# Mixture of experts by nested seven-product multiplication: the turn from P6 to P7 and P4 is put in another order, with operands and one weight sum kept on chip

## The chip, the cores and the metric

The kernel runs on one core of one Trainium2 chip. The metric is device time in microseconds (us) of one execution. The profile is a hardware trace of one execution; "PE" is the matrix engine (TensorE), "DVE" the vector engine, "ACT" the scalar engine, "POOL" GpSimd and "SP" the sync engine. ACT, POOL and SP also issue DMA transfers, each from its own queue of instructions, in order.

## The reference

Each of 8192 tokens (16 batches of 512) is multiplied with the weights of all eight experts, and the eight results are added with the softmax of the token's router logits as factors:

```python
    logits_max = np.max(router_logits, axis=-1, keepdims=True)
    probs = np.exp(router_logits - logits_max)
    probs = probs / np.sum(probs, axis=-1, keepdims=True)
    ...
    for e in range(n_experts):                      # 8 experts
        expert_out = np.matmul(x, expert_weights[e])    # [.., 512] x [512, 2048]
        output += probs[:, :, e:e+1] * expert_out
```

With the factors put on the tokens, this is one product of an 8192 x 4096 matrix (token times factor, for the 512 inputs of each of 8 experts) with a 4096 x 2048 matrix of all weights.

## The kernel before, in words

The large product is cut in two in each direction: the rows into even and odd blocks of 256 tokens, the inner dimension into experts 0 to 3 and 4 to 7, the columns into a left and a right half of 1024. Instead of eight block products the kernel makes seven (the scheme of Strassen in Winograd's form), named P1, P2, P5, P6, P7, P4 and P3 after the number `r` that `product(r, q)` takes. For each of them 16 row pairs `q` = 0 to 15 are worked through; a pair is the token blocks `a` = 2q and `b` = 2q + 1. Inside, each `Product` is cut in the same way once more, which gives seven steps of eight matmuls (`STEPS`: 1, 5, 6, 2, 7, 3, 4).

Left operands (class `Left`). Tiles `z` of 128 x 2048 elements, two for each product (`t[0]`, `t[1]`), are made on DVE. `times` multiplies a token block by factors; P6's left operand is P5's minus the block a's own; P7's is block a's product minus block b's (`first`, `second`, `less`: three instructions of DVE for each of two tiles, lines 433 to 453). Beside them a difference `d` (`queue_s2`) and a combination `i` (`queue_i`, queued when the stage begins) are made.

Right operands (class `Right`). Seven weight tiles of 1 MB, numbered by step. The weights of P7 and P4 are kept in DRAM (tiles `wd`): `by_parts` (line 1049) loads a quarter of the four raw blocks, makes the four sums 5, 7, 6 and 4 in place on DVE (`sums_in_place`, line 1010) and writes them back, four times for each. For P4 each raw block first has t2 subtracted (`less_t2`), and the difference is written back too before the sums run over it. `turnover` (line 1104) then fetches the seven tiles one by one from ACT's queue, three steps apart.

Results. A result tile `h` is 128 x 512 in f32. Four of them make up one product's result; each is added on DVE from a PSUM bank (or copied by ACT) and stored by POOL (`to_out`). P7 adds onto what P6 stored: `Base` loads the four tiles back from the output by SP's queue (`fetch_at` in line 911), the first three in the stage before their use and the fourth at step 3 of the stage itself. P4 then adds onto P7's tiles and lets the DMA accumulate into the output.

Order. `add` appends a stage of one or two products; a stage of two has 14 steps, in turns. The stages around the change are: (6, q) with (5, q + 1) for q = 1 to 14; then stage k7 with (6, 15) and (7, 0); then (4, q) with (7, q + 1) for q = 0 to 14; then k3 with (4, 15) and (3, 0). Work beside the matmuls is hung to a stage and a step by `at`. DVE's instructions are put in order by a planner: `later` appends a task with an estimated cost to a queue, `slack` runs tasks while the estimated time of DVE is behind that of PE, and `need` forces a task when a step reads it. DVE, ACT, POOL and SP execute what they are given in that order. Waits, and the choice of buffers, are put in by the framework; the pools hold 15 weight tiles (`w`), 8 `z`, 13 `h` and 9 of token blocks and factors (`xT`, `pT`). Each queue's DMA may wait for an earlier DMA, of this or another queue, that counts on the same semaphore.

Of the kernel before, what the change touches and what calls it, by code (L numbers as in the profile page):

```python
# [31 lines left out]
def kernel(  # L32
# [17 lines left out]
    C = H // P  # L50
# [60 lines left out]
    def tt(o, a, b, op):  # L111
        dve(nc.vector.tensor_tensor(out=o, in0=a, in1=b, op=op))  # L112
# [229 lines left out]
    class Task:  # L342


        def __init__(self, cost, make):
            self.cost, self.make, self.done = cost, make, False
# [79 lines left out]
    class Left:  # L426


        def __init__(self, xb, pb, less=None, of=None, part=None):
            self.xb, self.pb, self.less, self.of, self.part = xb, pb, less, of, part  # L430
            self.t, self.task, self.s2, self.i = [None, None], {}, None, None

        def makes(self, k):

            def first():
                if self.of is not None:
                    need(self.of.task[k])
                self.t[k] = new_z()
                times(self.t[k], k, self.xb, self.pb)

            def second():
                self.u = new_u()
                times(self.u, k, *self.less)

            def less():
                t = self.t[k]
                if self.of is not None:
                    tt(t, self.of.t[k], t, SUB)
                else:
                    tt(t, t, self.u if self.part is None else self.part.t[:, k], SUB)  # L450
            if self.less is not None:
                return first, second, less
            return (first, less) if self.of or self.part else (first,)
# [12 lines left out]
            self.task["s2"] = later(0.61, make)  # L466

        def queue_i(self):
            def make():
                self.i = new_z()  # L470
                two = "p k (h t) -> p h k t"
                tt(self.i.rearrange(two, h=2), self.t[1].rearrange(two, h=2),
                   self.s2.unsqueeze(1).to_broadcast([P, 2, K8, HP]), SUB)
            self.task["i"] = later(1.14, make)
# [174 lines left out]
    def out_rows(q, odd, cols, tn):  # L649
        t, n = tn  # L650
        return out_f[ds((2 * q + odd) * HQ + t * HP, HP), ds(cols * NH + n * NB, NB)]
# [26 lines left out]
    def add(*products):  # L678
        stages.append(products)
        return len(stages) - 1  # L680
# [7 lines left out]
    def xblock(h):  # L688
        if h not in xs:
            xs[h] = XBlock(h)  # L690
        return xs[h]

    def left_of(r, q, fresh=True):
        a, b = 2 * q, 2 * q + 1
        if r == 1:
            pt = PBlock(a, P1, xp1[q - 2][1] if q in (2, 3) else None)
            if q in (2, 3):
                xs[a] = XBlock(a, xp1[q - 2][0])
            return Left(xblock(a), pt), [xblock(a), pt]
        if r in (2, 4):  # L700
            h, pt = (a, PBlock(a, P2)) if r == 2 else (b, PBlock(b, P2))
            return Left(xblock(h), pt), [xblock(h), pt]
        if r == 5:
            pt = PBlock(b, PQ)
            return Left(xblock(b), pt), [xblock(b), pt]
        if r == 6:
            pt = PBlock(a, P1)
            return Left(xblock(a), pt, of=lefts[5, q]), [xblock(a), pt]
        if r == 3 and q in KEEP:
            pt = PBlock(a, P2)  # L710
            return Left(xblock(a), pt, part=Operand(lefts[6, q].kept)), [xblock(a), pt]
        pa, pb = PBlock(a, P1 if r == 7 else PQ), PBlock(b, P1 if r == 7 else PQ)
        return Left(xblock(a), pa, (xblock(b), pb)), [xblock(a), pa, xblock(b), pb]

# [2 lines left out]

    def product(r, q, **how):
        left, loads = left_of(r, q)
        lefts[r, q] = left  # L720
        p = None
        if r == 1:
            def sink(tn, o):
                pool(kept_rows(q)(tn), o)
            p = Product(right[1], left, sink)
        elif r == 2:
            if q >= 9:
                base = products[1, q].o.__getitem__
            else:
                base = bases[2, q] = Base(kept_rows(q))  # L730
            p = Product(right[2], left, to_out(q, 0, 0), base)
        elif r == 5:
            bases[6, q] = m1 = Base(kept_rows(q))
            m1.task = {}

            p = Product(right[5], left, to_out(q, 1, 0))
        elif r == 6:
            m1 = bases[6, q]

            def base(tn):  # L740
                need(m1.task[tn])
                return m1.t[tn]
            p = Product(right[6], left, to_out(q, 0, 1), base)
            if q in KEEP:
                left.kept = dram.tile([P, 2, K8, HQ], f16, name=f"kept_left_{q}")
        elif r == 7:
            base = bases[7, q] = Base(lambda tn: out_rows(q, 0, 1, tn))
            p = Product(right[7], left, to_out(q, 1, 1), base)
        elif r == 4:
            p = Product(right[4], left, to_out(q, 1, 0, accum_op=ADD), products[7, q].o.__getitem__)  # L750
        else:
            p = Product(right[3], left, to_out(q, 0, 1, accum_op=ADD), **how)
        p.loads = loads
        products[r, q] = p
        return p
# [21 lines left out]
                    load.store()  # L777

    def queue_left(left):
        if not left.task:  # L780
            left.queue_make(0)
            left.queue_s2()
            left.queue_make(1)

    thirds, splits, held = {}, {}, []

# [75 lines left out]
    def fetch_at(stage, slot, base, *tns):  # L862
        for tn in tns:
            at(stage, slot, lambda tn=tn: base.fetch(tn))
# [18 lines left out]
        add(product(6, q), product(5, q + 1))  # L883
    some = product(6, 15)
    xs.clear()
    k7 = add(some, product(7, 0))
    for q in range(15):
        add(product(4, q), product(7, q + 1))
    some = product(4, 15)
    xs.clear()  # L890
    k3 = add(some, product(3, 0))
    add(product(3, 14), product(3, 15))
# [1 line left out]
        add(product(3, q), product(3, q + 1))  # L894
    end = add(product(3, 13))
    late[k3 - 1] = 6

    def joined(q, tn):
        m1 = bases[6, q]
# [2 lines left out]
    for q in range(16):  # L902
        k = k5 + 1 + q
        duo = len(stages[k - 1]) == 2
        for slot, tn in zip((2, 4, 6, 8) if duo else (1, 2, 3, 4), INNER):
            fetch_at(k - 1, slot, bases[6, q], tn)
        for tn, where in zip(INNER, ((k - 1, 12), (k - 1, 13), (k - 1, 13), (k, 3)) if duo
                             else ((k - 1, 5), (k - 1, 6), (k - 1, 6), (k, 3))):
            at(*where, lambda q=q, tn=tn: joined(q, tn))
        for slot, tn in zip((7, 9, 11, 17), INNER):  # L910
            fetch_at(k7 + q - 1 + slot // 14, slot % 14, bases[7, q], tn)


    def wedge(kn, e):
# [92 lines left out]
            pool(kept_w("t4", ODD), made.pop(21))  # L1007
        later(2.2, make)

    def sums_in_place(part, b, r, cost):  # L1010

        def one(p, o, x, y):
            def make():
                tt(o, x, y, SUB)
                part(p, o)
            return later(cost, make)
        one(5, b[0, 0], b[0, 1], b[0, 0])
        one(7, b[0, 1], b[1, 1], b[0, 1])
        one(6, b[1, 1], b[1, 1], b[0, 0])
        return one(4, b[1, 0], b[1, 0], b[1, 1])  # L1020

    last2 = k5 - 1
    for stage, slot, q in ((9, 9, 12), (10, 2, 11), (10, 9, 22), (last2, 8, 21)):
# [25 lines left out]
    def by_parts(stage, slot, every, r, load, between, when):  # L1049

        for j in range(4):
            b, chunks = {}, ds(2 * j, 2)

            def begin(b=b, j=j, chunks=chunks):
                flush(last_part[0])
                t = new_w()
                for i, kn in enumerate(ORDER):
                    b[kn] = t[:, ds(2 * i, 2), :]
                    load(b[kn], kn, j, chunks)

            def go_on(b=b, chunks=chunks):
                for kn in b:
                    if kn != ODD:
                        between(b[kn], kn, chunks)

            def end(b=b, chunks=chunks):
                last_part[0] = sums_in_place(lambda p, o: pool(part_of((r, p), (0, 0), chunks), o), b, r, 0.61)
            at(*slots_after(stage, slot, j * every), begin)
            if between is not None:
                at(*slots_after(stage, slot, j * every + when[0]), go_on)  # L1070
            at(*slots_after(stage, slot, j * every + when[-1]), end)
# [23 lines left out]
        pool(part_of("b22", kn, chunks), t)  # L1095

    by_parts(k5 + 2, 4, 14, 7, load_part("t3"), None, (7,))
    by_parts(*slots_after(k5 + 2, 4, 60), 24, 4, load_p4, less_t2, (8, 15))
    by_parts(k7 + 4, 4, 36, 3, cast_part(22), keep_raw, (9, 16))


# [2 lines left out]
    def turnover(stage, place, r, raw):  # L1104
# [8 lines left out]
        at(stage - 1, 9, lambda: fetch(1))  # L1113
        for i, p in enumerate(STEPS[1:]):
            at(*slots_after(stage, place + 1, 3 * i), lambda p=p: fetch(p))
    turnover(k7 - 1, 1, 7, "t3")
    turnover(k7, 0, 4, "t4")
    turnover(k3 - 1, 1, 3, "b22")


# [94 lines left out]
```

## Time and profile before

| | us |
|---|---|
| median of three runs | 1374.11 |
| lowest and highest run | 1373.30 and 1378.75 |
| profiled execution | 1372.54 |
| its span, first to last instruction | 1370.8 |
| PE busy | 1362.6 (99%) |
| DVE busy | 1121.1 (82%) |
| POOL busy | 411.4 (30%) |
| ACT busy | 193.7 (14%) |

Between the span and the profiled execution's time lie 1.7 us. The 6610 matmuls are pipelined: one of 512 columns lasts 376 ns in the records, and the next begins before it has ended. Busy time of PE therefore tells that there was no gap, and the count of matmuls in a stretch tells the pace. The granted clock of TensorE is 1.000 over the span. A group of the costliest instructions carries line 112 or 132, since helpers issue all of DVE's and PE's; the tiles' names tell them apart.

### The profile page before, as it was taken

To read this page: it belongs to the slowest core of one execution; us is meant where nothing else is said; L and a number is where in the kernel's file an instruction comes from. 1 tells how busy PE (TensorE), PEld (TensorE's weight loads), DVE (VectorE), ACT (ScalarE), POOL (GpSimd) and SP (SyncE) were. 2 spreads that over 40 slices of the span, in tenths; PEclk is the share of its full clock that TensorE was granted. 3 is DMA by queue.
4 is the path that set the end of the run, shared out by engine and by line. 5 is a ranking of instruction groups with operands and counts; after the bars stand their busy time and mean duration, and the time that the engine had idled before them with its cause. 6 is when DMAs were issued, how large, how long until landed. Compare 5 with 4: busy or idle time off the path is not lost.

```text
span 1370.8 us, 18076 instructions
## 1 busy us (share of the span) xinstructions
PE 1362.6 (99%) x6610; PEld 644.1 (47%) x6610; DVE 1121.1 (82%) x1359; ACT 193.7 (14%) x354; POOL 411.4 (30%) x652
## 2 busy tenths in 40 slices
PE   8999999999999999999999999999999999999999
PEld 4455444444444444444444444444444444456554
DVE  5868757689889888798887978888889798997873
ACT  3232111100011111111111100000000000123321
POOL 3222333331223343343332112242332422233232
PEclk9999999999999999999999999999999999999999
DMA  9898999999897999999998999889797979999896
GB/s 182 217 223 245 208 237 283 233 323 358 235 340 245 323 295 332 286 318 315 306 296 289 364 371 258 200 236 209 227 264 216 242 212 282 309 209 241 203 207 121
DMA packets 193161, 358.50 MB, mean 262 GB/s; under 512 B 53168, under 2 KB 87216, under 8 KB 187696
## 3 DMA queue, kind: packets, MB, share of 16 engines
q0 software_dynamic: 88688, 185.12, 56.1%
q1 hardware_dynamic: 98336, 130.15, 31.3%
q10 hardware_dynamic: 6048, 42.08, 8.3%
q8 instruction: 51, 0.84, 0.2%
q14 instruction: 38, 0.31, 0.1%
HBM read 214.47 MB, written 170.07 MB: 281 GB/s over the span
## 4 chain that ended last, share of the span: by engine, by line
PE 74%; issue 11%; DMA 9%; POOL 4%; DVE 1%; ACT 0%; SPq 0%; POOLq 0%; DVEq 0%
PE ps L132 74%; DMA out_dram<-h 4%; POOL out_dram L126 2%; DMA wd<-w 2%; DMA xs<-in_x_dram 2%; DMA xT<-xs 1%; POOL wd L126 1%; POOL w L126 1%; DMA w<-in_expert_weights_dram 0%; DVE h L112 0%; DVE z L112 0%; POOL xs L126 0%; SPq L397 0%; POOLq L126 0%; DVE z L234 0%
## 5 line engine op out<-in xcount | busy, mean ns | idle before, releaser
L132 PE MATMUL ps<-w,z 128*128 128x512 f16 (+1 forms) x5272 | 1136.1, 376 | 1.7 <-DMA w<-in_expert_weights_dram 1.2
L132 PEld LDWEIGHTS <-z 128*128 128x128 f16 x5344 | 522.7, 98 | 607.2 <-DVE h L112 1.5
L126 POOL DMA_DIRECT2D out_dram<-h x380 | 249.1, 661 | 722.6 <-ACT h L559 365.4
L112 DVE TENSOR_TENSOR h<-ps,h 128x512 f32<-128x512 f32 x415 | 283.1, 686 | 177.1 <-PE ps L132 159.2
L112 DVE TENSOR_TENSOR z<-xT,pT 128x2048 f16<-128x2048 f16 x220 | 266.8, 1216 | 13.8 <-DMA xT<-xs 11.4
L132 PE MATMUL ps<-w,d 128*128 128x512 f16 x880 | 199.1, 379 | 0.4 <-DVE ps L112 0.4
L132 PEld LDWEIGHTS <-d 128*128 128x128 f16 x880 | 86.1, 98 | 102.5 <-issue 0.7
L112 DVE TENSOR_TENSOR z<-z,d 128x2048 f16<-128x2048 f16 x110 | 131.5, 1215 | 0.0
L112 DVE TENSOR_TENSOR w<-w 128x1024 f16<-128x1024 f16 (+2 forms) x92 | 100.7, 1102 | 9.2 <-DMA wd<-w 5.0
L559 ACT COPY h<-ps 128x512 f32<-128x512 f32 x64 | 37.5, 586 | 480.6 <-PE ps L132 458.8
L548 ACT COPY h<-ps 128x512 f32<-128x512 f32 x90 | 52.8, 586 | 326.5 <-PE ps L132 292.4
L112 DVE TENSOR_TENSOR d<-z 128x1024 f16<-128x1024 f16 x110 | 74.7, 686 | 7.6 <-PE ps L132 6.0
L112 DVE TENSOR_TENSOR ps<-ps,h 128x512 f32<-128x512 f32 (+1 forms) x102 | 60.3, 595 | 19.5 <-PE ps L132 19.3
L545 ACT COPY h<-ps 128x512 f32<-128x512 f32 x90 | 52.0, 589 | 151.7 <-PE ps L132 148.8
L126 POOL DMA_DIRECT2D wd<-w x86 | 48.6, 587 | 45.5 <-DVE w L112 34.7
L126 POOL DMA_DIRECT2D w<-in_expert_weights_dram x65 | 48.4, 761 | 28.0 <-DMA wd<-w 17.9
L126 POOL DMA_DIRECT2D kept<-h x56 | 30.8, 549 | 70.3 <-ACT h L548 40.0
L112 DVE TENSOR_TENSOR z<-z,u 128x2048 f16<-128x2048 f16 x38 | 46.1, 1214 | 0.1
L112 DVE TENSOR_TENSOR u<-xT,pT 128x2048 f16<-128x2048 f16 x38 | 46.2, 1215 | 0.0
L112 DVE TENSOR_TENSOR h<-h 128x512 f32<-128x512 f32 (+2 forms) x69 | 45.0, 674 | 0.1
L541 ACT COPY ps<-ps 128x512 f32<-128x512 f32 x45 | 25.6, 570 | 104.0 <-PE ps L132 98.2
L112 DVE TENSOR_TENSOR z<-z 128x2048 f16<-128x2048 f16 x32 | 39.0, 1220 | 0.6
(60 smaller groups left out, 262.8 us busy)
## 6 DMA issues: line engine op xcount, KB each, us to landing
out_dram<-h POOLq DMA_DIRECT2D x380, 256.0 KB, 6.7
pT<-p_dram SPq DMA_DIRECT2D x127, 256.0 KB, 6.5
w<-wd ACTq DMA_DIRECT2D x27, 1024.0 KB, 9.2
h<-kept SPq DMA_DIRECT2D x100, 256.0 KB, 7.9
xT<-x SPq DMA_DIRECT2D x74, 256.0 KB, 6.6
wd<-w POOLq DMA_DIRECT2D x72, 256.0 KB, 6.2
w<-in_expert_weights_dram POOLq DMA_DIRECT2D x35, 512.0 KB, 9.5
h<-out_dram SPq DMA_DIRECT2D x68, 256.0 KB, 5.5
```

Of the source, the lines that this page charges most:

```text
L112: dve(nc.vector.tensor_tensor(out=o, in0=a, in1=b, op=op))
L126: note(nc.gpsimd.dma_start(out=o, in_=i, **how))
L132: note(nc.tensor.matmul(ps, z, w, start=start, stop=stop, skip_group_check=True))
L541: act(nc.scalar.copy(self.banks["b"], x))
L545: act(nc.scalar.copy(o[tn], q if p == 5 else x))
L548: act(nc.scalar.copy(o[TN[p]], b if p == 2 else x))
L559: act(nc.scalar.copy(o[tn], b))
```

## The change

The diff moves and removes work around the turn to P7 and P4. PE's instructions are the same, in number and in shape.

1. Row pairs 14 and 15 come first in P7 and P4 (`order7`), ahead of 0 to 13, so that k7 holds (6, 15) and (7, 14), and the next stage (4, 14) and (7, 15). For these two pairs P7 adds onto P6's result tiles as they stand in SBUF (`products[6, q].o`), with no load of a base.
2. For these two pairs P7's left operand is made from P6's, in P6's own tiles (`into`): block b's token product for experts 4 to 7 goes into `u`, and P6's tile is subtracted from it in place. `queue_into` queues the first tile and the difference at step 6 of the stage before, the second tile is queued by `queue_i` when the stage begins.
3. For P7 and P4 `sums_in_place` makes three sums (5, 7, 6), not four. The fourth is made on chip from the fetched tiles 2 and 6 by `turnover_with_sums`, in two halves on DVE, ahead of the other tasks in the queue; six tiles are fetched rather than seven.
4. The quarters of P4's weights begin 28 steps apart, not 24, and their sums are queued 19 steps after the begin, not 15.

```diff
+            def all_of_it():
+                self.u = new_u()
+                times(self.u, k, self.xb, self.pb)
+
+            def less_in_place():
+                need(self.into.task[k])
+                t = self.t[k] = self.into.t[k]
+                tt(t, self.u, t, SUB)
+            if self.into is not None:
+                return all_of_it, less_in_place
...
         def queue_i(self):
+            if self.into is not None:
+                self.queue_make(1)
...
+        if r == 7 and q >= 14:
+            pt = PBlock(b, P2)
+            return Left(xblock(b), pt, into=lefts[6, q]), [xblock(b), pt]
...
         elif r == 7:
-            base = bases[7, q] = Base(lambda tn: out_rows(q, 0, 1, tn))
+            if q < 14:
+                base = bases[7, q] = Base(lambda tn: out_rows(q, 0, 1, tn))
+            else:
+                base = products[6, q].o.__getitem__
...
+    def queue_into(left):
+        left.queue_make(0)
+        left.queue_s2()
...
-    k7 = add(some, product(7, 0))
-    for q in range(15):
-        add(product(4, q), product(7, q + 1))
-    some = product(4, 15)
+    order7 = [14, 15, *range(14)]
+    k7 = add(some, product(7, order7[0]))
+    for q, next_q in zip(order7, order7[1:]):
+        add(product(4, q), product(7, next_q))
+    some = product(4, order7[-1])
...
+    for k, q in ((k7, 14), (k7 + 1, 15)):
+        at(k - 1, 6, lambda q=q: queue_into(lefts[7, q]))
...
-        for slot, tn in zip((7, 9, 11, 17), INNER):
-            fetch_at(k7 + q - 1 + slot // 14, slot % 14, bases[7, q], tn)
+        if q < 14:
+            for slot, tn in zip((7, 9, 11, 17), INNER):
+                fetch_at(k7 + q + 1 + slot // 14, slot % 14, bases[7, q], tn)
...
-        one(6, b[1, 1], b[1, 1], b[0, 0])
-        return one(4, b[1, 0], b[1, 0], b[1, 1])
+        sixth = one(6, b[1, 1], b[1, 1], b[0, 0])
+        return one(4, b[1, 0], b[1, 0], b[1, 1]) if all_ else sixth
...
-    by_parts(*slots_after(k5 + 2, 4, 60), 24, 4, load_p4, less_t2, (8, 15))
+    by_parts(*slots_after(k5 + 2, 4, 60), 28, 4, load_p4, less_t2, (8, 19))
...
+    def turnover_with_sums(stage, place, r, raw):
+
+        w = right[r].w = {}
+
+        def fetch(p):
+            w[p] = fetch_w(raw, RAW[p]) if p in RAW else fetch_w((r, p), (0, 0))
+
+        def sum_(p, x, y):
+            def make(e):
+                if e == 0:
+                    w[p] = new_w()
+                half_of = ds(e * C, C)
+                tt(w[p][:, half_of], w[x][:, half_of], w[y][:, half_of], SUB)
+            two = [later(1.14, lambda e=e: make(e), True) for e in (1, 0)]
+            right[r].task[p] = two[0]
+        at(stage - 1, 9, lambda: fetch(1))
+        for i, p in enumerate((5, 6, 2, 7, 3)):
+            at(*slots_after(stage, place + 1, 3 * i), lambda p=p: fetch(p))
+        at(*slots_after(stage, place, 18), lambda: sum_(4, 2, 6))
-    turnover(k7 - 1, 1, 7, "t3")
-    turnover(k7, 0, 4, "t4")
+    turnover_with_sums(k7 - 1, 1, 7, "t3")
+    turnover_with_sums(k7, 0, 4, "t4")
```

More of the change, by code (lines that the diff above doesn't have):

```diff
@@ L426, with __init__ @@
     class Left:
-        def __init__(self, xb, pb, less=None, of=None, part=None):
-            self.xb, self.pb, self.less, self.of, self.part = xb, pb, less, of, part
+        def __init__(self, xb, pb, less=None, of=None, part=None, into=None):
+            self.xb, self.pb, self.less, self.of, self.part, self.into = xb, pb, less, of, part, into
             self.t, self.task, self.s2, self.i = [None, None], {}, None, None
@@ L779, in queue_left @@
     def queue_left(left):
-        if not left.task:
+        if not left.task and left.into is None:
             left.queue_make(0)
@@ L1008, in odd_t4, with sums_in_place @@
         later(2.2, make)
-    def sums_in_place(part, b, r, cost):
+    def sums_in_place(part, b, r, cost, all_):
         def one(p, o, x, y):
@@ L1066, in end @@
             def end(b=b, chunks=chunks):
-                last_part[0] = sums_in_place(lambda p, o: pool(part_of((r, p), (0, 0), chunks), o), b, r, 0.61)
+                last_part[0] = sums_in_place(lambda p, o: pool(part_of((r, p), (0, 0), chunks), o), b, r, 0.61, r == 3)
             at(*slots_after(stage, slot, j * every), begin)
```

## The prediction

> **What bounds the kernel now.** First the page's span and busy times, then who PE waited for, then the matmul count in windows of time, and last the timeline at the two places where the count drops.
>
> ```profile
> span 1370.8 us, 18076 instructions
> ...
> PE 1362.6 (99%) x6610; PEld 644.1 (47%) x6610; DVE 1121.1 (82%) x1359; ACT 193.7 (14%) x354; POOL 411.4 (30%) x652
> ```
>
> Busy time of PE says only that no gap is seen, so the view of waits restricted to PE comes next (total us, times, longest):
>
> ```profile
> PE ps L132 <- ACT h L331: 1.4, 1, 1.4
> PE every L94 <- DVE zero L91: 1.3, 1, 1.3
> PE ps L132 <- DMA w<-in_expert_weights_dram: 1.2, 1, 1.2
> PE ps L132 <- DVE h L112: 0.5, 1, 0.5
> PE ps L132 <- DVE ps L112: 0.4, 1, 0.4
> ```
>
> The first three belong to the start (zeroing, first weights, early evacuation), which the change doesn't touch. The last two, 0.9 us in all, are everything else. Now the pace, in windows: four of 25 us, then three of the length of a stage, the first of them being k7 ((6, 15) with (7, 0), 778.8 to 802.7). Columns: window, its length, busy us and instructions in brackets for PE, PEld, DVE, ACT, POOL, then clock, DMA share, GB/s.
>
> ```profile
> 150.00:175.00 25.00, 25.00 (x118) 11.29 (x117) 16.70 (x19) 3.76 (x7) 8.22 (x14) 1.00 0.97 233
> ...
> 575.00:600.00 25.00, 24.90 (x116) 11.15 (x115) 20.47 (x28) 3.78 (x7) 11.54 (x20) 1.00 1.08 320
> ...
> 800.00:825.00 25.00, 24.14 (x112) 10.75 (x110) 18.10 (x22) 1.17 (x2) 5.29 (x10) 1.00 1.02 384
> ...
> 1050.00:1075.00 25.00, 25.00 (x118) 11.33 (x117) 21.08 (x26) 1.17 (x2) 8.60 (x12) 1.00 0.79 195
> ```
>
> ```profile
> 778.80:802.70 23.90, 23.90 (x113) 10.82 (x112) 20.35 (x25) 1.76 (x3) 4.28 (x8) 1.00 1.00 371
> 802.70:826.60 23.90, 23.04 (x107) 10.30 (x106) 18.90 (x23) 1.17 (x2) 3.35 (x5) 1.00 1.03 380
> 826.60:850.50 23.90, 23.90 (x113) 10.82 (x112) 20.59 (x25) 1.17 (x2) 7.20 (x11) 1.00 0.98 267
> ```
>
> Undisturbed windows hold 117 or 118 matmuls of 512 columns, whether DMA moves 195 or 233 GB/s and DVE is busy for 16.7 or 21.1 us: 25 / 117.3 = 0.213 us each, 1.705 us a step of eight, 23.9 us a stage of 14 steps. So PE's own pace is the bound, and only two places fall below it. In the stage after k7 107 matmuls stand where 112.5 belong: 5.5 x 0.213 = 1.2 us lost. At 575 to 600 about 1.3 are missing: 0.27 us. All that this change can win after the start is in these 1.5 us, since PE's 6610 matmuls stay.
>
> I weigh that against the Trainium skill. Its page "TensorE: Matmul & The Clock Gate", section "Back-to-back issue gap", gives about 131 ns for a sustained matmul of 512 columns and 216 ns for an isolated one; by the 131 ns PE would have hundreds of us to spare and another engine would bind. The trace, at granted clock 1.00, stands at 213 ns under any load, so the measurement decides for a saturated PE.
>
> **Where the 1.2 us come from.** Timeline of the stage's begin, all engines; brackets hold the idle time before and what ended it. The last row is PE's alone.
>
> ```profile
> 797.74 2.84 SPq L123 DMA_DIRECT2D h<-out_dram  x4
> ...
> 801.15 0.69 DVE L112 TENSOR_TENSOR h<-ps,h 128x512 f32<-128x512 f32 x1 [1.03 <-PE ps L132]
> ...
> 807.67 0.69 DVE L112 TENSOR_TENSOR h<-ps,h 128x512 f32<-128x512 f32 x1 [5.83 <-DMA out_dram<-h]
> 808.28 1.22 DVE L112 TENSOR_TENSOR z<-z,d 128x2048 f16<-128x2048 f16 x1
> ...
> 809.41 0.69 DVE L112 TENSOR_TENSOR ps<-ps,h 128x512 f32<-128x512 f32 x1
> 810.01 1.21 DVE L112 TENSOR_TENSOR z<-z,d 128x2048 f16<-128x2048 f16 x1
> ...
> 810.15 2.11 PE L132 MATMUL ps<-w,d 128*128 128x512 f16 x9 [0.41 <-DVE ps L112]
> ```
>
> ```profile
> 817.68 17.43 PE L132 MATMUL ps<-w,z 128*128 128x512 f16 x80 [0.45 <-DVE h L112]
> ```
>
> The add at 807.67 is the last of (7, 0): PSUM bank plus the fourth base tile. The row names a store of an `h` as releaser, but the operand that came last in the program is the fourth base: its load, planned for step 3 of k7 (778.8 + 3 x 1.7 = 784), is the first of the four issued by SP at 797.74, 9.9 us before the add. DVE stood 5.83 us, of which 1.2 reached PE, so DVE had some 4.6 us of cover. Who held SP, ACT and POOL there (the first row is from SP's own waits, 760 to 830 us; the others are ACT's and POOL's timelines):
>
> ```profile
> SPq L123 <- DMA pT<-p_dram: 24.5, 5, 14.9
> ```
>
> ```profile
> 782.54 13.02 ACTq L166 DMA_DIRECT2D w<-wd  x4
> 795.68 0.59 ACT L559 COPY h<-ps 128x512 f32<-128x512 f32 x1 [14.88 <-DMA w<-wd]
> 797.80 0.34 ACTq L166 DMA_DIRECT2D w<-wd  x1
> ```
>
> ```profile
> 796.56 0.54 POOL L126 DMA_DIRECT2D out_dram<-h  x1 [14.93 <-ACT h L559]
> 799.47 3.20 POOL L126 DMA_DIRECT2D out_dram<-h  x6 [2.37 <-ACT h L559]
> ```
>
> Each queue waited behind landings of the others while DMA moved 371 to 380 GB/s. Four weight fetches kept ACT for 13.02 us and made a result copy late, and POOL's stores behind that copy stood 14.93 us.
>
> **The change part by part.** Durations and landing times (median, us) come from these rows:
>
> ```profile
> L112 DVE TENSOR_TENSOR z<-xT,pT 128x2048 f16<-128x2048 f16 x220 | 266.8, 1216 | 13.8 <-DMA xT<-xs 11.4 <-DMA kept_left<-z 2.3
> ...
> L112 DVE TENSOR_TENSOR w<-w 128x1024 f16<-128x1024 f16 x60 | 40.7, 686 | 8.1 <-DMA wd<-w 5.0 <-DMA w<-in_expert_weights_dram 2.5
> ...
> L112 DVE TENSOR_TENSOR w<-w 128x2048 f16<-128x2048 f16 x12 | 14.6, 1213 | 0.0
> ```
>
> ```profile
> out_dram<-h POOLq DMA_DIRECT2D x380, 256.0 KB, 6.7
> ...
> w<-wd ACTq DMA_DIRECT2D x27, 1024.0 KB, 9.2
> ...
> wd<-w POOLq DMA_DIRECT2D x72, 256.0 KB, 6.2
> h<-out_dram SPq DMA_DIRECT2D x68, 256.0 KB, 5.5
> ```
>
> *Order of pairs and results in place.* Eight base loads go. Seven were hidden by the cover; the fourth of (7, 0) cost 1.2 us, and its place is taken by a tile that (6, 14) leaves in SBUF. New waits: P7 writes into a tile that P6's store must have read. By the changed program's order the closest is 8.6 steps from store to write, 14.7 us against a median landing of 6.7, and past 14.7 DVE's cover follows: price nothing. If POOL were again held 14.93 us, the write would wait 14.93 + 6.7 - 14.7 = 6.9 us, 2.3 beyond the cover; that's the upper end, but what held POOL is eased (next). Base loads for (7, 0) stand one stage after those of (7, 15), with the same lead as before, and later pairs keep their pattern. Gain 1.2 us.
>
> *Left operands in place.* (7, 14) and (7, 15) need two instructions a tile instead of three: 4 x 1.216 = 4.9 us of DVE less, and two loads each of `pT` and `xT` less on SP. DVE isn't on the path here, so no gain. The second tile of (7, 14) is now made when k7 begins: in the order it ends about 1.4 steps into k7 and PE reads it at step 7, 9 us of cover. PE's last read of P6's tile, step 12 of the stage before, is then past. Price nothing; if it were two instructions late, 2.3 us of that 9 would go.
>
> *Fourth weight sums.* Eight quarter sums (8 x 0.686 = 5.5 us), eight stores by POOL and two 1 MB fetches by ACT go; four sums of 2048 columns (4 x 1.213 = 4.9 us) come. With the loads above this is 20 x 256 KB + 2 x 1024 KB = 7.2 MB of transfer less, nearly all at the crowded turn. ACT loses one fetch of the four ahead of its copy at 795.68: 13.02 / 4 = 3.3 us earlier, and POOL's stores with it. The new wait: a sum stands in DVE's order, and all evacuations queue behind it. P7's reads tile 2, fetched 11.1 steps (19 us) ahead: against 9.2 covered. P4's sum stands 4.5 steps into the next stage, 802.7 + 7.7 = 810.4, and reads a tile that before was issued at 797.80: + 9.2 = 807.0, 3.4 us early, and 4.6 of cover behind that. In that stage I count 14 large and 15 small DVE instructions in the changed order; by the spacing in the timeline (1.13 and 0.60 us from start to start) that is 24.8 us in a stage of 23.9. k7 has 10 and 14, 19.7 us, so the 0.9 us is taken from 4.2 saved. Price nothing, with bounds of 0 and 0.9 for lost cover.
>
> *Quarters of P4's weights.* Timelines of POOL, DVE and PEld:
>
> ```profile
> 577.50 0.54 POOL L126 DMA_DIRECT2D wd<-w  x1
> ```
>
> ```profile
> 581.32 1.42 DVE L112 TENSOR_TENSOR w<-w 128x1024 f16<-128x1024 f16 x2 [3.97 <-DMA wd<-w]
> ```
>
> ```profile
> 583.39 8.30 PEld L132 LDWEIGHTS <-z 128*128 128x128 f16 x39 [0.38 <-issue]
> ```
>
> DVE's in-place sum waits till the raw block's store has landed; this makes the 0.27 us. The sums now come four steps (6.8 us) later, more than the 3.97 waited. All four quarters begin at the same step of a stage as this one. The last one ends 16 steps later than before; its stores are still some 7 steps (12 us) ahead of the fetch of P7's first tile, which reuses the buffer, against 6.2 to land. Gain 0.27.
>
> *Sum.* 1372.54 - 1.2 - 0.27 = 1371.1 for a profiled execution. The median of the runs shown lies 1.57 above that execution, so 1372.6.
>
> **Rivals.**
>
> *The loss stays or moves.* Queues so coupled can let another operand come late. For: DMA share is 1.0 at the turn. Against: every late operand I traced has its load removed or its queue shortened. Time 1374.1, between 1373 and 1376 (the 2.3 us above).
>
> *P4's fourth sum waits.* Place: DVE's second stage of the turn. If ACT is held once more for its 14.9 us, tile 2 lands at 797.8 + 14.9 + 9.2 = 821.9 and the sum stands 11.5 us, 6.9 beyond the cover. With the 1.5 won: +5.4, 1379.5. It decides from a landing after 815.0 us; over 0.5% slower (1381.0) from 823.4. Against: one fetch less, and in the changed order only SP loads issued early in the turn hold it. By the same page of the Trainium skill, section "HAM oscillation — how this bites in real kernels", a gap of PE over 3.4 us also halves the clock for a while, which would add to it; no run here shows that, the clock is 1.00 throughout and the longest gap 1.4 us.
>
> *DVE is the bound after all* (the 131 ns above taken at its word). Then its net 5.5 us (4.9 + 5.5 - 4.9) count in full: 1374.1 - 5.5 = 1368.6. The constant count of matmuls speaks against it.
>
> **How the numbers follow.** Forecast 0.64, the loss stays or moves 0.23, the sum waits 0.10, DVE binds 0.03. 0.5% is 6.9 us, about what a measurement of this kernel tells from no change. Only the worst of the sum's wait lies above it (0.04); below 1367.2 lies next to nothing (0.01); the rest is within, 0.95. The range runs from 1369.5 (DVE partly counted, or a median as near the profiled execution as the lowest run, 1373.3 - 1.5 = 1371.8, and some lower) to 1378.5, short of the waiting sum's full price; the forecast's own is 1371 to 1374.5, by the spread of lowest and median.
>
> **What would show it.** In the changed profile: the stage after k7 holds 112 or 113 matmuls, no add in it waits some 5 us on a DMA, 575 to 600 holds 117 or more, w<-wd counts 25, h<-out_dram 60, DVE is busy some 5 us less, ACT's hold in k7 is shorter than 14.9. A DVE wait on w<-wd at a `w<-w` of 128x2048 with PE idle behind it would prove me wrong.

## The result and the profile after

The changed kernel takes 1372.48 us (median of 13 runs, 1371.71 to 1375.37). The kernel before, run beside it and together with the runs known earlier, takes 1377.37 us (13 runs, 1373.30 to 1381.43). The ratio is 0.9968, 95% interval 0.9956 to 0.9980: 4.4 us faster (2.8 to 6.1), within the 0.5% that I had set as no change, and three times the 1.5 us of my sum. In a second series of runs (after_again, below) it is 0.9986 (0.9974 to 0.9998), 1.9 us, and there 1.5 us is not excluded. The fastest runs of both kernels lie close together (1371.6 for the kernel before among all its runs here, 1371.7 for the changed one); what differs is how often, and by how much, a run is slower than that.

The page's first lines and the rows of its DMA issues, of the changed kernel:

```profile
span 1370.5 us, 18024 instructions
...
PE 1361.9 (99%) x6610; PEld 644.0 (47%) x6610; DVE 1117.1 (82%) x1351; ACT 193.7 (14%) x354; POOL 407.1 (30%) x644
```

```profile
w<-wd ACTq DMA_DIRECT2D x25, 1024.0 KB, 9.3
...
h<-out_dram SPq DMA_DIRECT2D x60, 256.0 KB, 5.5
```

What PE waited for (total us, times, longest):

```profile
PE ps L132 <- DVE h L112: 1.8, 2, 1.6
PE ps L132 <- ACT h L331: 1.4, 1, 1.4
PE every L94 <- DVE zero L91: 1.3, 1, 1.3
PE ps L132 <- ACT h L653: 0.3, 1, 0.3
```

The 25 us window of P4's first quarter and the two stages of the turn (busy us and, in brackets, instructions of PE, PEld, DVE, ACT, POOL, then clock, DMA share, GB/s):

```profile
575.00:600.00 25.00, 25.00 (x118) 11.35 (x116) 20.77 (x28) 3.83 (x7) 7.92 (x15) 1.00 0.96 299
```

```profile
778.90:802.80 23.90, 23.90 (x113) 10.78 (x112) 20.62 (x25) 1.76 (x3) 4.05 (x9) 1.00 1.00 362
802.80:826.70 23.90, 23.90 (x112) 10.86 (x111) 22.25 (x26) 1.17 (x2) 4.91 (x8) 1.00 0.65 200
```

Both places are full: 118 matmuls where 116 stood, 112 where 107 stood. In the second stage DMA moves 200 GB/s at a share of 0.65, where it moved 380 at 1.03. ACT's timeline in k7, and POOL's store behind the copy:

```profile
779.25 2.04 ACTq L166 DMA_DIRECT2D w<-wd  x3
791.33 0.59 ACT L572 COPY h<-ps 128x512 f32<-128x512 f32 x1 [11.50 <-PE ps L132]
791.34 0.33 ACTq L166 DMA_DIRECT2D w<-wd  x1
```

```profile
792.21 0.54 POOL L126 DMA_DIRECT2D out_dram<-h  x1 [11.55 <-ACT h L572]
```

Three fetches leave ACT in 2.04 us, where four took 13.02. The result copy waits for PE alone and runs at 791.33 instead of 795.68, and the fetch of P4's tile 2 is issued at 791.34 instead of 797.80.

One new wait has come with the operands kept in place; a row of DVE's timeline:

```profile
809.77 0.69 DVE L112 TENSOR_TENSOR h<-ps,h 128x512 f32<-128x512 f32 x1 [1.00 <-DMA out_dram<-h]
```

This add of P7 writes into a result tile of P6 whose store, issued at 797.77, took 11.9 us to land. DVE stood 1.00 us; PE did not stop.

### The profile page after: what moved, and what is told of

Read it like the earlier page. It is cut to its first block, busy times and chain, and to the rows that moved or that the text cites. A ratio compares the mean times of both kernels' runs of the same rounds, so it can differ in the third digit from the quotient of the medians.

```text
span 1370.5 us, 18024 instructions
## 1 busy us (share of the span) xinstructions
PE 1361.9 (99%) x6610; PEld 644.0 (47%) x6610; DVE 1117.1 (82%) x1351; ACT 193.7 (14%) x354; POOL 407.1 (30%) x644
## 4 chain that ended last, share of the span: by engine, by line
PE 94%; DMA 3%; DVE 2%; issue 1%; ACT 0%; POOL 0%; SPq 0%; DVEq 0%; POOLq 0%
PE ps L132 93%; DMA w<-in_expert_weights_dram 1%; DMA out_dram<-h 1%; DMA xT<-xs 1%; DVE h L112 1%; DVE z L112 1%; DVE t L112 0%; PE every L94 0%; DVE s L112 0%; DVE z L234 0%; DVE d L112 0%; POOL w L126 0%; SPq L397 0%; DVE h L186 0%; DVE h L187 0%
## 5 line engine op out<-in xcount | busy, mean ns | idle before, releaser
L112 DVE TENSOR_TENSOR z<-xT,pT 128x2048 f16<-128x2048 f16 x216 | 262.2, 1217 | 15.5 <-DMA xT<-xs 15.5
L126 POOL DMA_DIRECT2D w<-in_expert_weights_dram x65 | 48.5, 762 | 19.6 <-DMA wd<-w 9.5
L126 POOL DMA_DIRECT2D wd<-w x78 | 44.2, 592 | 32.2 <-DVE w L112 25.8
L112 DVE TENSOR_TENSOR z<-z,u 128x2048 f16<-128x2048 f16 x34 | 41.4, 1216 | 0.1
```

The lines of the kernel that those rows point to most:

```text
L126: note(nc.gpsimd.dma_start(out=o, in_=i, **how))
```

## The experiments

All kernels of one group ran on one chip beside the kernel before; each group had another chip, so times compare within a group. The table holds medians, the ratio to the kernel before with its interval, and, from one trace of each, the matmuls in two stretches: 575 to 600 us (P4's first quarter; 117 or 118 when nothing is lost) and 755 to 830 us (the turn, the sum of three windows of 25 us; 352). One matmul missing is 0.213 us at the full clock. The first traces have 116 and 346 (kernel before) and 118 and 354 (changed kernel).

| kernel | us | ratio (95%) | 575-600 | 755-830 |
|---|---|---|---|---|
| *group 1, kernel before 1377.2* | | | | |
| before_again | 1375.3 | 0.9997 (0.9981-1.0013) | 103 | 353 |
| quarters_alone | 1380.8 | 1.0039 (1.0018-1.0060) | 117 | 326 |
| sum_alone | 1376.7 | 0.9997 (0.9982-1.0013) | 118 | 329 |
| order_alone | 1374.6 | 0.9993 (0.9978-1.0009) | 106 | 353 |
| *group 2, kernel before 1375.8* | | | | |
| order_undone | 1374.9 | 0.9992 (0.9979-1.0006) | 118 | 347 |
| sum_undone | 1373.4 | 0.9988 (0.9977-0.9999) | 112 | 354 |
| quarters_undone | 1373.5 | 0.9985 (0.9975-0.9995) | 117 | 351 |
| after_again | 1374.0 | 0.9986 (0.9974-0.9998) | 118 | 354 |
| *group 3, kernel before 1377.9* | | | | |
| quarters_alone_2 | 1380.9 | 1.0018 (1.0003-1.0034) | 115 | 318 |
| quarters_early_50 | 1377.6 | 0.9999 (0.9979-1.0019) | 118 | 354 |
| sums_later | 1379.9 | 1.0019 (0.9998-1.0041) | 118 | 346 |
| sum_early | 1374.3 | 0.9982 (0.9965-0.9999) | 117 | 337 |

**The kernel before, traced again.** No edit.

> The kernel before, unchanged, under a second name, for another trace of it. Over 13 runs it stands at 1377.4 us, 4.9 above the changed kernel and 4.8 above the one execution whose trace I predicted from. Theory A (the recorded sum: 1.2 us at the turn and 0.27 at P4's first quarter, in every execution): the trace again shows about 1.5 us of lost matmul time after the start, and the rest of the 4.9 is not in the change. Theory B (the same two places lose more in a common execution): this trace shows 3 to 6 us of lost matmul time, nearly all of it at the quarters of P4's weights or at the turn. Ratio to the kernel before 1.000 within 0.0015.

Its trace, in windows and in PE's timeline:

```profile
575.00:600.00 25.00, 22.38 (x103) 9.94 (x102) 21.64 (x29) 2.92 (x5) 10.95 (x19) 1.00 0.99 337
...
805.00:830.00 25.00, 25.00 (x118) 11.32 (x116) 20.27 (x25) 1.17 (x2) 4.99 (x8) 1.00 1.02 366
```

```profile
576.82 17.55 PE L132 MATMUL ps<-w,z 128*128 128x512 f16 x80 [1.72 <-DVE h L112]
595.27 3.61 PE L132 MATMUL ps<-w,d 128*128 128x512 f16 x16 [0.90 <-DVE ps L112]
```

This execution lost 14.3 x 0.213 = 3.0 us at the first quarter, where the first trace had lost 0.27, and nothing at the turn, where the first trace had lost 1.2. The same program, the same places, other sizes: the loss depends on when transfers land, and that differs from execution to execution. Theory B, at its lower edge, holds against A in this. The first trace came from one of the kernel's fastest executions (1372.54, against a median of 1377); this one, of 1374.87, is faster than the median too, and no execution near the median was traced.

At the quarter two operands were late here, as DVE's timeline shows:

```profile
572.47 0.69 DVE L112 TENSOR_TENSOR h<-h 128x512 f32<-128x512 f32 x1 [3.46 <-DMA h<-kept]
...
588.04 0.69 DVE L112 TENSOR_TENSOR w<-w 128x1024 f16<-128x1024 f16 x1 [1.93 <-DMA wd<-w]
```

The wait for a raw block's store (`wd<-w`), which the prediction names, stands before PE's gap of 0.90 us. The larger gap, 1.72 us, comes before any of these sums: DVE had waited 3.46 us for the load of a kept result (`h<-kept`), and ran without a pause from there to the add that released PE.

**Each part alone.** The quarters' times:

```diff
-    by_parts(*slots_after(k5 + 2, 4, 60), 24, 4, load_p4, less_t2, (8, 15))
+    by_parts(*slots_after(k5 + 2, 4, 60), 28, 4, load_p4, less_t2, (8, 19))
```

> The kernel before with P4's quarters 28 steps apart and their four sums 19 steps after the begin; nothing else. Theory A: 0.3 us less than before (ratio 0.9998). Theory B with the loss at the quarters: 3 us or more less (0.998 or lower). Theory C (what counts is the transfer that goes, 7.2 MB): no difference, since it moves none.

The fourth sum on chip:

```diff
-        return one(4, b[1, 0], b[1, 0], b[1, 1])
+        return one(4, b[1, 0], b[1, 0], b[1, 1]) if all_ else sixth
...
-    turnover(k7 - 1, 1, 7, "t3")
-    turnover(k7, 0, 4, "t4")
+    turnover_with_sums(k7 - 1, 1, 7, "t3")
+    turnover_with_sums(k7, 0, 4, "t4")
```

> The kernel before with the fourth sum of P7's and P4's weights made on chip; order, operands and quarters' times as before. Theory A: no difference (0 to 0.3 us, since it takes one sum from the quarters' group). Theory B: part of the loss at the turn (up to 1.2 us) goes, since ACT fetches one tile less there. Theory C: 4 of the 7.2 MB go with it, so more than half of the gain, 2.5 us or more (0.998).

The order of pairs, with results and left operands in place:

```diff
-        for slot, tn in zip((7, 9, 11, 17), INNER):
-            fetch_at(k7 + q - 1 + slot // 14, slot % 14, bases[7, q], tn)
+        if q < 14:
+            for slot, tn in zip((7, 9, 11, 17), INNER):
+                fetch_at(k7 + q + 1 + slot // 14, slot % 14, bases[7, q], tn)
...
+    order7 = [14, 15, *range(14)]
+    k7 = add(some, product(7, order7[0]))
...
+            if self.into is not None:
+                return all_of_it, less_in_place
```

> The kernel before with pairs 14 and 15 first in P7 and P4, P6's results and left operands taken in place; four sums stored and the quarters' times as before. Theory A: 1.2 us less (0.9991) and the loss at the turn gone from the trace. Theory B with the loss at the turn: 3 us or more less (0.998 or lower). Theory C: 3 of 7.2 MB, 2 us less.

No part alone wins anything that can be measured, and one loses, which none of the theories had: the quarters' times cost 0.39%, 5.4 us. Its windows at the turn, and PE's and ACT's timelines:

```profile
755.00:780.00 25.00, 24.68 (x114) 10.92 (x113) 21.04 (x24) 3.50 (x6) 4.30 (x8) 1.00 0.99 346
780.00:805.00 25.00, 24.11 (x112) 10.77 (x110) 23.34 (x30) 1.17 (x2) 3.24 (x6) 1.00 1.01 398
805.00:830.00 25.00, 21.73 (x100) 9.80 (x101) 16.18 (x19) 1.76 (x3) 5.19 (x9) 1.00 1.03 400
```

```profile
805.72 8.81 PE L132 MATMUL ps<-w,z 128*128 128x512 f16 x40 [1.61 <-DMA w<-wd]
...
823.99 2.32 PE L132 MATMUL ps<-w,z 128*128 128x512 f16 x10 [2.55 <-DVE h L112]
```

```profile
784.95 0.59 ACT L548 COPY h<-ps 128x512 f32<-128x512 f32 x1 [13.53 <-DMA out_dram<-h]
784.98 10.53 ACTq L166 DMA_DIRECT2D w<-wd  x4
```

26 matmuls (5.5 us) are missing over the turn, and here PE itself waited for a weight tile. Its fetch is the third of the four that ACT issued after standing 13.53 us for a store's landing; issued at 786.08, it took 19.6 us to land (the median of `w<-wd` was 9.2 in the first trace), with DMA at 398 GB/s in that window. At the first quarter nothing is lost (117).

order_alone shows the reverse in its trace: the turn is clean, the first quarter is not.

```profile
575.00:600.00 25.00, 23.04 (x106) 10.21 (x105) 20.41 (x27) 3.50 (x6) 9.51 (x17) 1.00 0.96 316
...
805.00:830.00 25.00, 25.00 (x117) 11.37 (x116) 20.79 (x26) 1.17 (x2) 5.14 (x9) 1.00 0.83 307
```

sum_alone keeps the base loads, and its trace has the wait that the prediction had read into the turn, this time under its own name; DVE's timeline, PE's and a window:

```profile
811.46 0.69 DVE L112 TENSOR_TENSOR h<-ps,h 128x512 f32<-128x512 f32 x1 [8.87 <-DMA h<-out_dram]
```

```profile
813.94 5.30 PE L132 MATMUL ps<-w,d 128*128 128x512 f16 x16 [3.46 <-DVE ps L112]
```

```profile
810.00:830.00 20.00, 16.54 (x70) 7.08 (x68) 18.48 (x22) 1.17 (x2) 2.86 (x4) 0.91 0.73 225
```

DVE stood 8.87 us for the fourth base tile, and 23 matmuls are missing over the turn. So the fetch that goes does not by itself free the turn, and theory C (a gain in proportion to the transfer saved; 0.998 for this part) fails with 0.9997, 0.9982 to 1.0013, for 4 of 7.2 MB.

**Each part undone.** The same edits, taken out of the changed kernel one at a time; of the first two the main lines are shown.

```diff
...
-    order7 = [14, 15, *range(14)]
-    k7 = add(some, product(7, order7[0]))
+    k7 = add(some, product(7, 0))
...
```

> The changed kernel with the old order of pairs, left operands and base loads (so the fourth sum on chip and the quarters' times stay). Theory D, formed from the four runs with one part each: a common execution of the kernel before loses some 3 us at P4's first quarter and 1 to 2 at the turn; moving the quarters cures the first and, as their end comes 16 steps nearer to the turn, makes the turn worse unless the turn's own loads go. By D this kernel stands at 1376 to 1380 us, with its loss between 760 and 830 us and none at 575 to 606. Theory A (parts add up: 0.27 and 0): 1376.9, as before. Theory C (transfers): two thirds of the gain, 1374.

```diff
...
-    turnover_with_sums(k7 - 1, 1, 7, "t3")
-    turnover_with_sums(k7, 0, 4, "t4")
+    turnover(k7 - 1, 1, 7, "t3")
+    turnover(k7, 0, 4, "t4")
...
```

> The changed kernel with all four sums made by quarters and stored, seven tiles fetched (so order, operands in place and the quarters' times stay). Theory D: both losses cured, 1372.5 to 1374 us; if the seventh fetch still crowds the turn, 1 to 2 us lost at 780 to 830. Theory C: 3 of 7.2 MB saved, 1375.3.

```diff
-    by_parts(*slots_after(k5 + 2, 4, 60), 28, 4, load_p4, less_t2, (8, 19))
+    by_parts(*slots_after(k5 + 2, 4, 60), 24, 4, load_p4, less_t2, (8, 15))
```

> The changed kernel with P4's quarters 24 steps apart and their sums 15 steps after the begin, as before (so order, operands in place and the fourth sum on chip stay). Theory D: the turn is clean, and some 1 to 3.5 us are lost at 575 to 606, where DVE waits for the raw blocks' stores: 1373.5 to 1376 us. Theory A: 0.27 above the changed kernel, 1372.8. Theory C: all of the transfer is saved, 1372.5.

> The changed kernel, unchanged, for another trace and on the same chip as the three above. All theories: 1372.5 us, 0.9968 of the kernel before within 0.0015, and no matmul time lost at 575 to 606 and at 780 to 830.

One window of each at the turn, in this order:

```profile
805.00:830.00 25.00, 23.84 (x112) 10.70 (x111) 19.85 (x23) 1.17 (x2) 5.47 (x9) 1.00 0.94 329
```

```profile
805.00:830.00 25.00, 25.00 (x118) 11.29 (x117) 23.26 (x28) 1.17 (x2) 6.06 (x9) 1.00 0.85 276
```

```profile
805.00:830.00 25.00, 25.00 (x117) 11.37 (x116) 24.07 (x28) 1.17 (x2) 5.76 (x9) 1.00 0.70 211
```

```profile
805.00:830.00 25.00, 25.00 (x118) 11.33 (x117) 24.82 (x29) 1.17 (x2) 5.70 (x8) 1.00 0.68 205
```

The three with the new order are at 0.9985 to 0.9988 and full at the turn; without it the ratio's interval holds 1, and the turn still loses (5 matmuls, 1.1 us). The four intervals overlap, so it is the traces more than the times that set the order apart. With the new order either other part can be left out with no measurable difference. after_again was expected at 0.9968 within 0.0015 and came out at 0.9986, a smaller gain than forecast.

The times of order_undone decide neither for D nor for A. Both were given in us against 1377.4, and the kernel before stands at 1375.8 here; as ratios, A's 1.000 lies in the interval of 0.9979 to 1.0006, D's 0.999 to 1.002 overlaps it, and C's 0.9975 lies just outside. Its trace shows what D says: nothing lost at the quarter, a loss at the turn. With the fourth sum on chip the late quarters cost nothing that can be measured. That suggests that what made quarters_alone slow is the late quarters together with the four sums' extra stores and fetch; the two ran on different chips, so it isn't shown.

Undoing the quarters lost nothing at 575 to 606 in its one trace, against D's 1 to 3.5 us; sum_undone, with the quarters moved, lost 1.1 us there. So the quarters' move doesn't cure that place reliably, and its absence doesn't always cost. The rows of sum_undone tell why: the late operand is again the load of a kept result, which the move of the sums doesn't touch. DVE's timeline and PE's:

```profile
572.02 0.69 DVE L112 TENSOR_TENSOR h<-h 128x512 f32<-128x512 f32 x1 [3.06 <-DMA h<-kept]
```

```profile
576.36 17.43 PE L132 MATMUL ps<-w,z 128*128 128x512 f16 x80 [1.05 <-DVE h L112]
```

**Why the quarters alone are slower.** quarters_alone once more, then with the first quarter at step 50:

```diff
-    by_parts(*slots_after(k5 + 2, 4, 60), 28, 4, load_p4, less_t2, (8, 19))
+    by_parts(*slots_after(k5 + 2, 4, 50), 28, 4, load_p4, less_t2, (8, 19))
```

> The kernel before with the quarters' times alone, once more, beside the three below. If its loss is the kernel's and not that of the chip it ran on: 1.003 to 1.006 of the kernel before, lost between 760 and 830 us. If it was the chip's: 1.000 within 0.0015.

> As quarters_alone, but the first quarter begins at step 50, not 60, so that the last one ends 6 steps later than in the kernel before, not 16. Theory D (the later end of the quarters crowds the turn): most of the slow-down is gone, 1.0015 or lower. Rival E (28 steps apart and sums at 19 cost by themselves, wherever they end): 1.003 to 1.006 as quarters_alone.

```diff
-    by_parts(*slots_after(k5 + 2, 4, 60), 24, 4, load_p4, less_t2, (8, 15))
+    by_parts(*slots_after(k5 + 2, 4, 60), 24, 4, load_p4, less_t2, (8, 19))
```

> The kernel before with P4's sums queued 19 steps after a quarter's begin, not 15; quarters 24 steps apart as before, so the last one ends 4 steps later. Theory D (the loss at 575 to 606 is DVE's wait for the raw blocks' stores): no loss there in the trace, and 0.9985 to 0.9998 of the kernel before, the loss at the turn staying. Rival E: slower than before, 1.001 to 1.004.

The loss repeats on another chip, smaller (1.0018), with 34 matmuls missing at the turn. Ten steps earlier it is 0.9999, and the turn is full in the trace (but the first quarter, now in 550 to 575 us, lost 20 matmuls); windows of 20 us hold 94 when nothing is lost:

```profile
780.00:800.00 20.00, 20.00 (x95) 9.05 (x93) 19.58 (x24) 1.17 (x2) 2.17 (x4) 1.00 1.02 415
800.00:820.00 20.00, 20.00 (x94) 9.08 (x93) 12.74 (x17) 1.17 (x2) 3.92 (x8) 1.00 1.03 382
```

That speaks for D: the later end crowds the turn. It isn't settled by the times, whose intervals overlap, and the rate of transfer is about the same here as in quarters_alone (398 and 400); which landing decides at the turn stays open. D's expectation for sums_later failed, and its median, 1.0019, lies where rival E had it, with 1 inside the interval. The first quarter is clean as D has it, but other quarters now lose:

```profile
575.00:600.00 25.00, 25.00 (x118) 11.33 (x117) 20.97 (x28) 3.52 (x7) 8.82 (x16) 1.00 1.03 319
655.00:680.00 25.00, 24.69 (x113) 10.96 (x112) 20.73 (x27) 3.50 (x6) 7.14 (x13) 1.00 1.08 288
700.00:725.00 25.00, 23.20 (x109) 10.43 (x108) 17.09 (x22) 4.09 (x7) 6.50 (x12) 1.00 1.11 298
805.00:830.00 25.00, 24.15 (x112) 10.77 (x111) 19.11 (x23) 1.17 (x2) 4.07 (x8) 1.00 1.03 385
```

From 545 to 735 us DVE no longer waits for a store of a raw block in this trace. It waits for loads; the longest, 5.20 us for `h<-kept` at 719.34, stands ahead of the largest loss. So the later sums remove the wait that the prediction named, and others break the pace instead.

**The price of the slower rival.** In the changed kernel the queueing of P4's fourth sum is moved from 18 to 8 steps:

```diff
-    turnover_with_sums(k7, 0, 4, "t4")
+    turnover_with_sums(k7, 0, 4, "t4", 8)
```

> The changed kernel with P4's fourth sum queued 8 steps into the turn, not 18, so that it stands in DVE's order before its tile 2 has landed: the price of the slower rival of the prediction. In the changed kernel's trace that tile landed at 798.8 and the sum would now stand at about 793.2, so DVE waits some 5.6 us and then makes two halves (2.3 us) ahead of the results. If 4.6 us of cover is right, 1 to 3.5 us of matmul time is lost there: 1.0007 to 1.0025 of the changed kernel, 0.999 to 1.001 of the kernel before. If there is no cover, 5 us or more; if the tile's landing is earlier in a common execution, nothing.

DVE's and PE's timelines:

```profile
802.39 2.36 DVE L112 TENSOR_TENSOR w<-w 128x2048 f16<-128x2048 f16 x2 [6.19 <-DMA w<-wd]
```

```profile
805.40 6.86 PE L132 MATMUL ps<-w,z 128*128 128x512 f16 x31 [2.56 <-DVE h L112]
```

DVE stood 6.19 us, then made the two halves, 2.36 us, and PE stood 2.56. So 3.6 us were covered if the wait alone is counted, and 6.0 if the halves, now ahead of the results, count as delay; the 4.6 of the prediction lies between. The changed kernel didn't run on this chip, so the price in the median isn't known. Seven of the twelve runs took 1372.8 to 1374.3 us and five 1377.2 to 1381.8, the traced one (1377.95) among the latter; that the tile lands earlier in the first seven is likely and not shown.

## Why the prediction was right, and where it wasn't

**The bound held.** PE's pace is 0.213 us a matmul of 512 columns in every undisturbed window of every kernel here, and PE's instructions didn't change. The fastest runs of the two kernels are 0.1 us apart (1371.6 and 1371.7), so nothing but lost matmul time could be won.

**The two places were right, their size was not.** "All that this change can win after the start is in these 1.5 us" is the step that failed. It took the losses of one execution, and a fast one, for those of the kernel. Another execution of the kernel before lost 3.0 us at the quarter and none at the turn. The median run lies 4 to 6 us above the fastest of its series. The forecast of 1372.6 came out at 1372.48 nevertheless, because I took the saving from a median of 1374.11, of three runs, that more runs moved to 1377.37; from that median the same sum gives 1375.9. That the level was right to 0.1 us is luck: the saving was 4.4 us in one series and 1.9 in the other, not 1.5. Where a median run of the kernel before loses the rest isn't shown, since the two traced executions are faster than that.

**The turn.** The late fourth base was the right operand. The row in sum_alone names it, and in the first trace, whose row names a store, its load took 9.8 us from 797.74 to land, 0.1 us before the add at 807.67. Putting P6's results in its place is what the gain seems to need: in every trace with the new order the turn is full, but for sum_early, where the early sum is in the way; both kernels with it and one other part are faster than the kernel before, and every kernel without it has 1 in its interval or is slower. Alone it isn't measurable (0.9993, 0.9978 to 1.0009), its one trace having lost 2.4 us at the quarter, 0.9 at 675 to 700 us, and more at the start and at 118 us, ahead of anything that the edit touches. ACT's fetches came free by more than the 3.3 us that I had worked out: the copy by 4.35, the fetch of tile 2 by 6.5.

**New waits at nothing.** Right for PE. Neither sum waited; the row of the two tiles' sums has no idle time before it:

```profile
L112 DVE TENSOR_TENSOR w<-w 128x2048 f16<-128x2048 f16 x16 | 19.5, 1216 | 0.0
```

The second stage ran through with DVE busy 22.25 us of 23.9, where I had reckoned 24.8. The write into P6's tile did wait: I had 14.7 us from store to write against a landing of 6.7, and it was 11.0 against 11.9. The 1.00 us stayed inside DVE's cover, in this trace alone of those with the new order. DVE's busy time fell by 4.0 us (1121.1 to 1117.1), not by the 5.5 of instructions removed; and the rival that DVE is the bound is out by the pace of PE.

**The quarters.** The term of 0.27 us was wrong in kind. The wait that it names is real, but the larger part of the loss in the kernel's second trace came from a late `h<-kept`, which the edit leaves as it is. And I priced the end of the last quarter by its distance to one fetch (12 us against 6.2 to land), and found it covered; that the same 16 steps bring its transfers nearer to the turn, where the DMA share is at 1.0 already, I left out; quarters_early_50 points to it without settling it. Alone the move costs 2.5 to 5.4 us. In the changed kernel it neither costs nor wins anything measurable.

**The rivals.** The sum's wait didn't come; where the sum was queued too early it stopped PE for 2.56 us in one trace. That a long gap of PE also lowers its clock, as the Trainium skill's page "TensorE: Matmul & The Clock Gate" states, section "HAM oscillation — how this bites in real kernels", is shown by other runs (below).

## What to carry to other kernels

Where the bounding engine is full and only late transfers break its pace, one trace shows where the loss can be, not how large it is: run the kernel a dozen times, and take the distance of the median from the fastest run as the most that can be won (here 4 to 6 us, of which the change won 1.9 to 4.4). A schedule that moves transfers has to be judged at every crowded place that they move towards, not only at the wait that they leave; and a part that costs time alone can be free once another part has emptied that place. And a schedule edit cures only the operand that it moves: at the quarter a load that it left alone was late too. Here the traces point to the operands kept in place at the crowded turn as the part that counts; the times alone don't separate it from the others.

## What the runs showed that I hadn't expected

The clock. After the gap of 3.46 us in sum_alone, 16 matmuls took 5.30 us, not 3.62, and the granted clock of that window is 0.91. In quarters_alone_2 a gap of 3.29 us did the same. That agrees with the 3.4 us of the Trainium skill's page for the first, nearly for the second. But in quarters_early_50 the clock fell after 2.55 us; a window and PE's timeline:

```profile
560.00:580.00 20.00, 20.00 (x86) 8.76 (x85) 17.55 (x22) 3.50 (x6) 4.53 (x8) 0.91 1.07 327
```

```profile
559.79 8.54 PE L132 MATMUL ps<-w,z 128*128 128x512 f16 x31 [2.55 <-DVE h L112]
```

Two gaps of the same length didn't lower it (quarters_alone at 823.99 with 2.55 us, sum_early at 805.40 with 2.56). So one stall of 2.5 to 3.5 us can cost some 1.7 us more, and the limit isn't a fixed 3.4 us in these traces.

The spread of one program's runs was the other surprise: 1371.6 to 1381.1 us for the kernel before on one chip; the changed kernel's 13 runs stayed within 3.7 us. Not all of it lies in what the change touches. The windows from 10 to 15 us of the changed kernel's two traces, in this order, and PE's timeline in the second:

```profile
10.00:15.00 5.00, 5.00 (x49) 3.25 (x47) 1.85 (x3) 1.42 (x3) 2.04 (x3) 1.00 1.28 227
```

```profile
10.00:15.00 5.00, 4.46 (x26) 2.80 (x27) 1.35 (x2) 0.81 (x2) 1.48 (x2) 0.67 1.28 227
```

```profile
10.54 2.48 PE L132 MATMUL ps<-w,z 128*128 128x512 f16 x8 [2.88 <-DMA w<-in_expert_weights_dram]
```

The first weights came later, the clock fell, and the same matmuls stand 2.5 us later from there on. That accounts for the difference between the two spans (1370.5 and 1372.9 us); at the quarter and at the turn neither lost anything. The traces of order_alone, order_undone and quarters_undone start in the same way.
